# Two places each for the two rotary result tiles, and their high parts as pairs in the pool of the gate's and the convolution's tiles

## The chip, the cores and the metric

One core of a Trainium2 chip runs the whole layer as one program. The metric is the device time of one launch in microseconds (us). The engines are TensorE (PE: matmuls; PEld: its weight loads), VectorE (DVE), ScalarE (ACT), GpSimd (POOL) and SyncE (SP), which here only issues DMAs. Each engine works its instructions off in program order, so an instruction that waits holds up all that stand behind it on its engine. That also holds for DMA issues on SP's queue and on POOL's.

## The reference, cut to what matters

The layer normalizes the input (1024 tokens, 1024 wide), projects it, runs a gated linear attention (GLA) on one half of the columns and a differential attention on the other, joins both by an output projection, then a convolutional feed-forward block, a gated embedding and a last norm. The change lies where queries and keys of the differential attention get their rotary embedding:

```python
def rope(x, pos):
    d = x.shape[-1]
    inv_freq = ROPE_THETA ** (-jnp.arange(0, d, 2, dtype=jnp.float32) / d)
    ang = pos.astype(jnp.float32)[..., None] * inv_freq
    cos, sin = jnp.cos(ang)[:, :, None, :], jnp.sin(ang)[:, :, None, :]
    x1, x2 = xf[..., : d // 2], xf[..., d // 2:]
    return jnp.concatenate([x1 * cos - x2 * sin, x2 * cos + x1 * sin], axis=-1)

q = (rope(q.reshape(B, T, H * 2, dqk), pos) * (dqk ** -0.5)).reshape(B, T, H, 2, dqk)
k = rope(k.reshape(B, T, H * 2, dqk), pos).reshape(B, T, H, 2, dqk)
```

## The kernel before

Every float32 product is made of three matmuls: each operand is split into a high part (rounded to float32r) and a low part (the rest), and `mm3` adds high by high, high by low and low by high.

**A block.** `fm(k, h, evict)` projects the columns of weight block k for half h of the tokens: 24 matmuls (8 slices of 128 rows, three each) into one PSUM tile `psd`, of which there are two. Block n therefore starts only after DVE has read block n - 2.

**A round.** `rotary` (line 534) treats one group of heads (`pr`), queries or keys (`qk`) and one half of the tokens (`h`) at a time: eight rounds, called rounds 1 to 8 here. A round has two blocks, x1 and x2. Of the first, DVE makes `rt0 = x1 cos` (L546) and `rt1 = x1 sin` (L547); of the second `rt2 = x2 sin` (L550) and `rt3 = x2 cos` (L551). POOL makes `rt0 - rt2` in place of rt0 (L552) and `rt3 + rt1` in place of rt3 (L553). These two are the results. ACT rounds each to its high part `rh0`, `rh1` (L560 for queries, L562 for keys), and SP stores it to DRAM (L563); DVE makes the low part in the result's own place (L568, L571), and SP stores that (L572). A round so has four stores of 256 KB, in the order rh0, low part of rt0, rh1, low part of rt3, each to a piece of DRAM of 4 x 32 rows of 512 numbers.

**Places.** rt0, rt2, rt3 and rh0 have one place, rt1 and rh1 share two: six tiles of 2 KB per partition. A tile with one place can be written only when the store of what was in it has landed.

**Weights.** Two raw tiles take the weights from DRAM (L195, 512 KB per block, 20 loads); ACT casts them (L272), DVE makes the low part (L274). The load for block k + 2 is issued when DVE has read block k. Block numbers 4 to 11 are the rounds', 12 to 15 the output gate's, 16 to 19 those of the V projection.

**The gate.** After the rounds, for each of four heads two blocks (k = 12 to 15, halves 0 and 1) give z (L854); ACT applies silu (L861), DVE multiplies with the GLA result `on` (L862), which had been stored to DRAM and is loaded back (L845) into a tile of the tag `c`, of which there are two of 4 KB per partition. The convolution uses this tag much later. ACT and DVE split the product (L866, L867).

**What sets the order.** PE, ACT, DVE and POOL keep the order in which a planner (`Line`, with costs per operation, due times and priorities) calls them. It knows nothing of places. SP's order is set by the tile framework, which places a DMA by when its tile comes free. POOL also issues the loads of the attention's heads (L818, L821), right behind its last L553.

Of the kernel before, what the change touches and what calls it, by code (L numbers as in the profile page):

```python
# [9 lines left out]
F32 = mybir.dt.float32  # L10
F32R = mybir.dt.float32r
# [7 lines left out]
P = 128  # L19
# [24 lines left out]
HALF = 512  # L44
# [85 lines left out]
def kernel(ctx: ExitStack, tc: tile.TileContext, a, out, dbg=None):  # L130
# [17 lines left out]
    wp = ctx.enter_context(tc.tile_pool(name="wp", bufs=2))  # L148
# [37 lines left out]
    wcnt = [0]  # L186
# [39 lines left out]
    with ExitStack() as ph:  # L226
        ph.enter_context(tc.manual_schedule(engines={pe.engine, act.engine, dve.engine, pool.engine}))
        r1 = ph.enter_context(tc.tile_pool(name="r1", bufs=1, side="right"))
# [29 lines left out]
        def prepare(k, delay=3.0, after=()):  # L258

            if k >= len(order) + 4 or k < len(wts):  # L260
                return
            i = k - len(order)
            shape = [P, KB, P] if i < 0 else [P, 2, HALF]
            raw = raw_tile(a["wfm"][order[k]] if i < 0 else a["wtm"][1, i], shape)
            hl = []
            wts.append(hl)

            def hi():
                for nm in ("wh", "wl"):
                    wcnt[0] += 1  # L270
                    hl.append(wp.tile(shape, F32R, name=f"{nm}{wcnt[0]}", tag="w", bufs=8))
                act.copy(hl[0], raw)  # L272
            k_ = line.op("A", T, hi, 2, after, delay)
            line.op("V", T, lambda: dve.tensor_sub(hl[1], raw, hl[0].bitcast(F32)), 2, (k_,), key=("wf", k))  # L274
# [3 lines left out]
        def fm(k, h, evict):  # L278

            n = nf[0]  # L280
            nf[0] += 1
            if n > 1:
                line.need(("fm", n - 2))
            line.need(("wf", k))
            wh, wl = wts[k]
            ps = pd.tile([P, HALF], F32, name="psd", tag="d")
            for kb in range(KB):
                mm3(ps, wh[:, kb], wl[:, kb], xs(xh[h], kb), xs(xl[h], kb), kb == 0, kb == KB - 1)
                line.step(0.69)
                if kb < KB - 1:  # L290
                    yield
            evict(ps, ("fm", n))
            yield
# [224 lines left out]
        with ExitStack() as gs:  # L518
# [15 lines left out]
            def rotary(pr, qk, k):  # L534

                dst = (qs_d, ks_d)[qk]
                for h in range(2):
                    cs = slice(h * HALF, (h + 1) * HALF)
                    t = {}

                    def new(i, t=t):
                        t[i] = r1.tile([P, HALF], F32, name=f"rt{i}", bufs=(1, 2, 1, 1)[i])
                        return t[i]

                    def ev_a(ps, key, t=t, cs=cs, new=new):
                        k_ = line.op("V", HALF, lambda: dve.tensor_mul(new(0), ps, cosr[:, cs]), 1, (("cos",),))  # L546
                        line.op("V", HALF, lambda: dve.tensor_mul(new(1), ps, sinr[:, cs]), 1, (k_,), key=key)  # L547

                    def ev_b(ps, key, t=t, cs=cs, new=new):
                        k1 = line.op("V", HALF, lambda: dve.tensor_mul(new(2), ps, sinr[:, cs]), 1)  # L550
                        line.op("V", HALF, lambda: dve.tensor_mul(new(3), ps, cosr[:, cs]), 1, (k1,), key=key)  # L551
                        ka = line.op("G", HALF, lambda: pool.tensor_sub(t[0], t[0], t[2]), 1, (k1,))  # L552
                        kb_ = line.op("G", HALF, lambda: pool.tensor_add(t[3], t[3], t[1]), 1, (key,))  # L553
                        for x, i, k_ in ((0, 0, ka), (1, 3, kb_)):
                            r_ = {}

                            def hi(x=x, i=i, r_=r_):
                                r_["h"] = r1.tile([P, HALF], F32R, name=f"rh{x}", tag=("rh0", "rt1")[x], bufs=(1, 2)[x])
                                if qk == 0:
                                    act.activation(r_["h"], t[i], AF.Copy, scale=0.125)  # L560
                                else:
                                    act.copy(r_["h"], t[i])  # L562
                                sp.dma_start(dst[4 * pr:4 * pr + 4, 0, x, :, cs], r_["h"].bitcast(F32))  # L563

                            def lo(x=x, i=i, r_=r_):
                                rl = t[i].bitcast(F32R)
                                if qk == 0:
                                    dve.scalar_tensor_tensor(out=rl, in0=t[i], scalar=0.125, in1=r_["h"].bitcast(F32),  # L568
                                                             op0=ALU.mult, op1=ALU.subtract)
                                else:  # L570
                                    dve.tensor_sub(rl, t[i], r_["h"].bitcast(F32))  # L571
                                sp.dma_start(dst[4 * pr:4 * pr + 4, 1, x, :, cs], rl.bitcast(F32))  # L572
                            k_ = line.op("A", HALF, hi, 1, (k_,))
                            line.op("V", HALF, lo, 2, (k_,))
                    prepare(k + 2 + h)
                    yield from fm(k, h, ev_a)
                    yield from fm(k + 1, h, ev_b)
# [1278 lines left out]
    def gate(h, c0, c1, fb, st):  # L1856

        W = c1 - c0
        ng[0] += 1
        if ng[0] > 5:  # L1860
            line.need(("g", ng[0] - 5))
        line.need(("gw", fb))
        if fb % 2 == 0:
            st["pr", fb] = xt([P, 2, HALF], F32)[:, :, 0:W]
            sp.dma_start(st["pr", fb], pp_d[h, fb // 2][:, :, c0:c1])
        psg = pg.tile([P, HALF], F32, name="psg", tag="g")[:, 0:W]
        for kb in range(KB):
            line.need(("v", h, kb))
            vh, vl = vv[h][kb // 2]
            mm3(psg, wg[fb][0][:, kb], wg[fb][1][:, kb], vh[:, kb % 2, c0:c1], vl[:, kb % 2, c0:c1],  # L1870
                kb == 0, kb == KB - 1)
            line.step(W * 3 / 2400)
        return psg, ("g", ng[0])
# [86 lines left out]
    with tc.manual_schedule(engines={pool.engine}):  # L1960
# [38 lines left out]
        for fb in range(4, KB):  # L1999
            x = gate(*part, fb, st)  # L2000
# [90 lines left out]
```

## Time and profile before

| | us |
|---|---|
| median of 3 runs | 1408.72 (1407.35 to 1412.62) |
| the profiled execution: time, span | 1407.91, 1406.0 |
| PE busy in it | 1342.6 |
| DVE, ACT, POOL busy | 922.5, 619.6, 153.1 |
| rounds 1 to 8, first L546 to last | 145.0 to 283.5 |
| gate blocks, end of the last on PE | 330.7 |

The profiled execution lies 0.8 us under the median. PE is the busiest engine, yet a busy PE is not a fast one: matmuls run at the clock that was granted, and the profile gives that clock by stretch. Busy shares are means over stages; which wait ends last in a stage is told by the chain of waits and by the timelines of single engines.

### The profile page before, as it was taken

How to read it: one execution, taken by the hardware profiler on the slowest of the kernel's cores; microseconds unless marked ns; L12 is line 12 of the kernel's file. 1: busy time of each engine (PE TensorE's matmuls, PEld its weight loads, DVE VectorE, ACT ScalarE, POOL GpSimd, SP SyncE). 2: the span in 40 equal slices, each digit the busy share in tenths (PEclk: the TensorE clock that was granted, in tenths of full speed). 3: DMA queues.
4: the chain of work that ended last, by engine and by line, in shares of the span. 5: the costliest groups of instructions: out<-in, count | busy, mean ns of one | idle time of the engine just before them, and what ended most of it. 6: DMA issues, size and time to landing. Idle time of an engine off the chain costs nothing.

```text
span 1406.0 us, 16439 instructions
## 1 busy us (share of the span) xinstructions
PE 1342.6 (95%) x6335; PEld 1076.0 (77%) x6335; DVE 922.5 (66%) x1307; ACT 619.6 (44%) x947; POOL 153.1 (11%) x176
## 2 busy tenths in 40 slices
PE   9999998899999999988999999999999999999996
PEld 6777676676777787756788888888887888887896
DVE  8455653435776777598877778777775363258576
ACT  7434431124664668444554544444554121025444
POOL 0100111120211112320000000000000000013231
PEclk9999999999999999998999999999999999999999
DMA  6101323361658346320222222122275143021222
GB/s 232 31 31 45 98 76 105 96 194 59 190 185 242 118 161 218 123 76 16 90 80 85 90 91 77 73 80 85 91 280 183 61 152 119 15 75 46 83 98 75
DMA packets 49757, 151.87 MB, mean 108 GB/s; under 512 B 5360, under 2 KB 11920, under 8 KB 49680
## 3 DMA queue, kind: packets, MB, share of 16 engines
q1 hardware_dynamic: 45072, 135.10, 28.5%
q0 software_dynamic: 4608, 15.73, 4.2%
q8 instruction: 49, 0.80, 0.2%
q14 instruction: 28, 0.23, 0.0%
HBM read 108.87 MB, written 41.94 MB: 107 GB/s over the span
## 4 chain that ended last, share of the span: by engine, by line
PE 74%; DMA 10%; DVE 9%; ACT 4%; issue 2%; POOL 1%; SPq 1%; DVEq 0%; ACTq 0%; POOLq 0%
PE psu L1441 29%; PE psu L135 14%; PE psg L135 5%; PE psd L135 5%; PE psw L135 4%; PE s L135 3%; PE gps L135 3%; DMA ks_d<-rt 2%; PE psf L135 2%; DMA qs_d<-rt 2%; PE oat L135 2%; PE pst L135 2%; DMA raw<-in_wtm 1%; PE o L135 1%; PE psp L135 1%
## 5 line engine op out<-in xcount | busy, mean ns | idle before, releaser
L1441 PE MATMUL psu<-xt,wt 128*128 128x512 f32 x1008 | 236.9, 390 | 0.0
L1441 PEld LDWEIGHTS psu<-xt,wt 128*128 128x128 f32 x1008 | 189.4, 188 | 40.6
L135 PE MATMUL psd<-xt,wh 128*128 128x512 f32 x512 | 170.8, 416 | 17.7 <-DVE rt L547 12.9
L135 PEld LDWEIGHTS psd<-xt,wh 128*128 128x128 f32 x512 | 96.8, 195 | 44.8 <-issue 14.1
L1441 PE MATMUL psu<-yt,yt 128*128 128x512 f32 x480 | 115.9, 391 | 0.0
L1481 DVE SCALAR_TENSOR_TENSOR c<-s,cwt,c 128x1023 f32<-128x1023 f32 (+1 forms) x88 | 109.2, 1280 | 4.5 <-ACT c L1478 1.9
L1634 DVE TENSOR_TENSOR yt<-yt,psu 128x512 f32<-128x512 f32 x64 | 43.8, 688 | 102.4 <-PE psu L135 102.4
L1441 PEld LDWEIGHTS psu<-yt,yt 128*128 128x128 f32 x480 | 90.0, 188 | 19.4 <-DVE yt L969 0.2
L135 PE MATMUL psd<-xt,wl 128*128 128x512 f32 x256 | 102.8, 401 | 0.0
L135 PE MATMUL psu<-xt,wt 128*128 128x512 f32 x384 | 95.0, 398 | 3.2 <-ACT xt L1620 2.0
L135 PEld LDWEIGHTS psu<-xt,wt 128*128 128x128 f32 x384 | 74.0, 193 | 19.5 <-ACT xt L1620 2.4
L1559 DVE TENSOR_TENSOR s<-s,psu 128x512 f32<-128x512 f32 x60 | 41.1, 686 | 67.9 <-PE psu L1441 67.5
L1551 ACT COPY s<-psu 128x512 f32<-128x512 f32 x80 | 47.0, 588 | 64.1 <-PE psu L1441 60.4
L1776 POOL TENSOR_TENSOR wg<-raw,wg 128x1024 fp32r<-128x1024 f32 x2 | 4.8, 2402 | 627.7 <-ACT wg L1774 627.7
L1478 ACT ACTIVATE c<-s,cwt 128x1024 f32<-128x1024 f32 x44 | 54.8, 1247 | 39.3 <-DVE s L1559 33.7
L1441 PE MATMUL psu<-yt,d 128*128 128x512 f32 x264 | 66.2, 401 | 5.8 <-DVE yt L1385 5.1
L967 ACT CAST wt<-raw 128x1024 fp32r<-128x1024 f32 x42 | 44.3, 1056 | 59.7 <-DVE raw L993 38.2
L1441 PEld LDWEIGHTS psu<-yt,d 128*128 128x128 f32 x264 | 50.7, 193 | 18.3 <-DVE yt L1385 5.5
L1094 ACT ACTIVATE p<-s,nb 128x128 f32<-128x128 f32 (+7 forms) x64 | 47.5, 742 | 30.2 <-DVE nb L1102 28.4
L1102 DVE TENSOR_REDUCE nb<-s 128x1 f32<-128x128 f32 (+7 forms) x64 | 48.3, 755 | 17.6 <-PE s L135 17.2
L135 PEld LDWEIGHTS psd<-xt,wl 128*128 128x128 f32 x256 | 50.1, 196 | 11.2
L135 PE MATMUL psw<-yt,wt 128*128 128x512 f32 x192 | 52.5, 408 | 0.9 <-DVE dvt L1059 0.9
(359 smaller groups left out, 2667.0 us busy)
## 6 DMA issues: line engine op xcount, KB each, us to landing
d<-in_w_up SPq DMA_DIRECT2D x42, 512.0 KB
g_d<-c SPq DMA_DIRECT2D x22, 512.0 KB
raw<-in_w_down SPq DMA_DIRECT2D x22, 512.0 KB
raw<-in_wfm SPq DMA_DIRECT2D x16, 512.0 KB
s<-g_d SPq DMA_DIRECT2D x16, 512.0 KB
yt<-h_d SPq DMA_DIRECT2D x12, 512.0 KB
yt<-ks_d POOLq DMA_DIRECT2D x16, 256.0 KB, 10.3
xt<-ks_d POOLq DMA_DIRECT2D x16, 256.0 KB, 8.0
```

The costliest lines, as they stand in the source:

```text
L135: return pe.matmul(o, l, r, start=start, stop=stop)
L967: act.copy(hl[0], src())
L1094: act.activation(p[:, 0:W], s[:, 0:W], AF.Exp, bias=nb, accum_out=ssum[:, mp:mp + 1])
L1102: k_ = line.op("V", W, lambda: dve.tensor_reduce(out=nb, in_=s[:, 0:W], op=ALU.max, axis=AX.X, negate=True), 2)
L1441: pe.matmul(ps, l[:, c + kb], r[:, kb % 2], start=(kb, i) == (0, 0) and not more, stop=(kb, i) == (3, 2), skip_group_check=more)
L1478: act.activation(c_[i], S[n, i], AF.Identity, scale=cwt[:, blk, 2:3], bias=cwt[:, blk, 3:4])
L1481: k_ = line.op("V", T * 1.05, lambda d=d: dve.scalar_tensor_tensor(out=c_[i][:, d:T], in0=S[n, i][:, 0:T - d], scalar=cwt[:, blk, 2 - d:3 ...
L1551: act.copy(S[n, i][:, lo:lo + HALF], ps)
L1559: dve.tensor_add(o, o, ps)
L1634: line.op("V", HALF, lambda: dve.tensor_add(hblk(h, fb), hblk(h, fb), ps), 0, key=key)
L1776: line.op(lo_eng, T, lambda: (pool if lo_eng == "G" else dve).tensor_sub(wg[fb][1], raws[fb], wg[fb][0].bitcast(F32)), 3, (k_,), key=("gw" ...
```

## The change

The tiles rt0 and rt3 get two places each. rt1 no longer shares with rh1 and gets one, rt2 keeps one: six places as before. The high parts leave this pool: a round takes one tile of tag `c`, 2 x 512 numbers per partition, and rh0 and rh1 are its halves. The tag keeps its two places, which the gate's `on` tiles use too.

```diff
-                        t[i] = r1.tile([P, HALF], F32, name=f"rt{i}", bufs=(1, 2, 1, 1)[i])
+                        t[i] = r1.tile([P, HALF], F32, name=f"rt{i}", bufs=(2, 1, 1, 2)[i])
...
-                                r_["h"] = r1.tile([P, HALF], F32R, name=f"rh{x}", tag=("rh0", "rt1")[x], bufs=(1, 2)[x])
+                                if x == 0:
+                                    wcnt[0] += 1
+                                    t["h"] = wp.tile([P, 2, HALF], F32R, name=f"rh{wcnt[0]}", tag="c", bufs=2)
+                                r_["h"] = t["h"][:, x]
```

Lines behind the diff move by three (L568 becomes L571, L571 becomes L574, L572 L575, L845 L848). The order of PE, DVE, ACT and POOL is the same, instruction by instruction; what differs there are the waits. On DVE, in round 2 before (rt_1463 and rt_1547 are its two results; a DMAHW semaphore is that of a DMA that SP issued):

```order
L546 TENSOR_TENSOR rt_1463<-psd,cosr 128x512 [waits DMAHW5_49,DVE_49,PE_49]
L568 SCALAR_TENSOR_TENSOR rt_1325<-rt_1325,rh_1374 128x512 [waits Pool_49]
L547 TENSOR_TENSOR rt_1471<-psd,sinr 128x512
L550 TENSOR_TENSOR rt_1536<-psd,sinr 128x512 [waits PE_49]
L551 TENSOR_TENSOR rt_1547<-psd,cosr 128x512 [waits DMAHW7_49]
```

The same in the changed kernel:

```order
L546 TENSOR_TENSOR rt_1462<-psd,cosr 128x512 [waits PE_49]
L571 SCALAR_TENSOR_TENSOR rt_1325<-rt_1325,rh_1345 128x512 [waits Pool_49]
L547 TENSOR_TENSOR rt_1470<-psd,sinr 128x512
L550 TENSOR_TENSOR rt_1535<-psd,sinr 128x512 [waits PE_49]
L551 TENSOR_TENSOR rt_1546<-psd,cosr 128x512
```

In round 2 the waits for the stores of round 1 are gone; from round 3 on L546 and L551 wait for the stores of the round before the last.

On SP, the end of the rounds and the loads behind it, before (raw_2263 and raw_2330 are weight blocks 16 and 17, on_2257 the gate's third head; on_2110 and on_2174, the first two, stand far ahead, before the first rh store):

```order
L195 DMA raw_2192<-in_wfm 128x1024
L572 DMA ks_d<-rt_2021 4x32x512
L563 DMA ks_d<-rh_2092 4x32x512
L572 DMA ks_d<-rt_2061 4x32x512
L563 DMA ks_d<-rh_2097 4x32x512
L572 DMA ks_d<-rt_2088 4x32x512
L195 DMA raw_2263<-in_wtm 128x1024
L195 DMA raw_2330<-in_wtm 128x1024
L845 DMA on_2257<-on_d 128x1024
```

The same place in the changed kernel (raw_2255 and raw_2322 are blocks 16 and 17; rh_2085 is the pair of round 8, rt_2015 the second result of round 7):

```order
L195 DMA raw_2184<-in_wfm 128x1024
L575 DMA ks_d<-rt_2015 4x32x512
L848 DMA on_2102<-on_d 128x1024
L566 DMA ks_d<-rh_2085 4x32x512
L575 DMA ks_d<-rt_2054 4x32x512
L566 DMA ks_d<-rh_2085 4x32x512
L575 DMA ks_d<-rt_2081 4x32x512
L195 DMA raw_2255<-in_wtm 128x1024
L848 DMA on_2166<-on_d 128x1024
L195 DMA raw_2322<-in_wtm 128x1024
L848 DMA on_2249<-on_d 128x1024
```

The loads of `on` for the first two heads now stand among the last stores: on_2102 waits until round 7's pair is stored, on_2166 until round 8's is.

## Rows read from the trace of the kernel before

**Rows 1.** The page: the chain that ended last, by engine and line

```profile
PE 74%; DMA 10%; DVE 9%; ACT 4%; issue 2%; POOL 1%; SPq 1%; DVEq 0%; ACTq 0%; POOLq 0%
PE psu L1441 29%; PE psu L135 14%; PE psg L135 5%; PE psd L135 5%; PE psw L135 4%; PE s L135 3%; PE gps L135 3%; DMA ks_d<-rt 2%; PE psf L135 2%; DMA qs_d<-rt 2%; PE oat L135 2%; PE pst L135 2%; DMA raw<-in_wtm 1%; PE o L135 1%; PE psp L135 1%
```

**Rows 2.** The chain, 140 to 340 us: start, length, what

```profile
167.06 6.84 DMA qs_d<-rt
...
215.56 13.20 DMA ks_d<-rt
...
280.24 10.14 DMA ks_d<-rt
...
295.81 19.97 DMA raw<-in_wtm
...
319.52 11.15 PE psd L135 x48
```

**Rows 3.** Timeline of DVE: start, length, operation, idle before and its end

```profile
174.03 0.69 DVE L546 TENSOR_TENSOR rt<-psd,cosr 128x512 f32<-128x512 f32 x1 [4.97 <-DMA qs_d<-rt]
...
267.91 0.69 DVE L546 TENSOR_TENSOR rt<-psd,cosr 128x512 f32<-128x512 f32 x1 [3.88 <-DMA qs_d<-rt]
...
275.96 0.69 DVE L551 TENSOR_TENSOR rt<-psd,cosr 128x512 f32<-128x512 f32 x1 [6.17 <-DMA qs_d<-rt]
...
283.47 0.69 DVE L546 TENSOR_TENSOR rt<-psd,cosr 128x512 f32<-128x512 f32 x1 [3.38 <-DMA ks_d<-rt]
...
309.69 1.23 DVE L862 TENSOR_TENSOR on<-on,yt 128x1024 f32<-128x1024 f32 x1 [1.13 <-ACT yt L861]
316.95 1.23 DVE L274 TENSOR_TENSOR wl<-raw,wh 128x1024 fp32r<-128x1024 f32 x1 [6.03 <-ACT wh L272]
```

**Rows 4.** Timeline of PE, the same columns

```profile
176.57 1.14 PE L135 MATMUL gms<-gsq,ones_r 128*128 128x512 f32 x2 [3.25 <-DVE on L754]
...
220.44 0.73 PE L135 MATMUL psd<-xt,wh 128*128 128x512 f32 x2 [2.19 <-DVE rt L547]
...
319.52 0.70 PE L135 MATMUL psd<-xt,wh 128*128 128x512 f32 x2 [0.81 <-DVE yt L854]
```

**Rows 5.** SP's issues: start, length, transfer

```profile
210.20 0.51 SPq L563 DMA_DIRECT2D ks_d<-rh  x1
...
277.28 0.51 SPq L572 DMA_DIRECT2D ks_d<-rt  x1
...
280.24 0.91 SPq L572 DMA_DIRECT2D ks_d<-rt  x1
...
293.59 0.51 SPq L563 DMA_DIRECT2D ks_d<-rh  x1
```

**Rows 6.** Windows: length, busy of PE, PEld, DVE, ACT, POOL; clock, DMA share, GB/s

```profile
176.57:186.54 9.97, 9.97 (x40) 7.26 (x41) 5.89 (x10) 2.49 (x5) 1.81 (x5) 0.66 0.19 52
144.76:151.84 7.08, 6.91 (x41) 4.93 (x40) 5.42 (x10) 2.49 (x5) 0.80 (x4) 1.00 0.55 186
229.00:233.00 4.00, 3.31 (x15) 2.75 (x16) 3.98 (x4) 0.62 (x1) 1.67 (x1) 1.00 0.15 26
246.30:249.00 2.70, 2.70 (x13) 2.25 (x12) 2.05 (x2) 0.63 (x1) 0.37 (x1) 1.00 0.22 30
249.00:261.70 12.70, 8.65 (x37) 6.60 (x36) 3.69 (x6) 1.58 (x2) 2.31 (x2) 1.00 0.36 117
261.70:264.00 2.30, 2.30 (x11) 1.88 (x11) 2.30 (x2) 0.63 (x1) 0.65 (x1) 1.00 0.22 27
277.30:280.00 2.70, 2.70 (x13) 2.22 (x12) 2.70 (x2) 0.62 (x1) 1.11 (x1) 1.00 0.17 20
285.00:291.70 6.70, 6.10 (x26) 4.75 (x27) 1.59 (x3) 0.62 (x1) 1.75 (x2) 1.00 0.26 91
292.70:295.50 2.80, 2.80 (x14) 2.32 (x13) 1.64 (x2) 2.54 (x3) 2.80 (x6) 1.00 0.23 36
295.50:316.50 21.00, 21.00 (x94) 17.39 (x93) 7.75 (x10) 5.18 (x7) 2.99 (x8) 1.00 0.95 255
```

## The prediction

> **What bounds the kernel now.** I read the chain of waits on the page first. Nearly all of it is TensorE, with two entries of 2% each that are stores of the rotary results [rows 1]: about 56 of 1406 us in which the end of the program hangs on a DMA. The chain in order of time shows where. One piece lies in round 2, at 167 us. Then five follow one another, one per round, from 215.56 to 280.24 us, of 10 to 13 us each, and behind them stands the load of weight block 16 with 20 us [rows 2]. DVE's timeline shows what the stores hold: L546 and L551 stand idle until a store has landed, since rt0 and rt3 have one place [rows 3]. PE waits little by that view, some 2 us at a time, for L547 or L551 [rows 4], but two blocks take it 11.15 us (48 matmuls at full clock) [rows 2], and a round took 15.6 us (from L546 at 267.91 to the next at 283.47 [rows 3]). So PE could go faster by 4.4 us a round if nothing else stood in the way.
>
> Whether something does is to be read from the windows. Between the raw loads the DMA share is flat at 0.26 with 91 GB/s while stores run [rows 6]. A queue that sends on all 16 engines would show more; 0.25 is four of 16. So the stores run on a quarter of the DMA engines, and "26% busy" is full for them. The four stores of a round and its raw load took 12.7 us in a busy stretch (249.0 to 261.7); then come 2.3 to 4 us in which the share is 0.15 to 0.23 but only 20 to 36 GB/s flow, five times after 229 us [rows 6]. These gaps are the start of a store on an empty queue: rt0's low part is issued at 277.28 [rows 5], and bytes flow from 280.0 on. 12.7 and 2.7 make up the round's 15.6. The stage is thus bound by the store queue, and a part of this bound is that the queue runs dry once per round.
>
> The Trainium skill says the same of the quarter ("DMA: Bandwidth & Descriptors", section "Why a DMA increments its semaphore by 16 and not by 1"): a DMA uses the largest number of engines up to 16 that divides the outermost sizes, which for a destination of 4 x 32 x 512 is 4. The trace agrees with 0.26.
>
> **The change part by part.** Nothing is added to or taken from PE, DVE, ACT or POOL, and no transfer is added. What changes are waits, and SP's order.
>
> *Round 2.* L546 waits no longer (4.97 us on DVE [rows 3]). Behind it on DVE stands the L754 that PE's `gms` waits for: 3.25 us of PE [rows 4]. After that wait PE's clock was at its lower level: 40 PE instructions took 9.97 us at a mean clock of 0.66, the like stretch of round 1 took 7.08 us at 1.00 [rows 6]: 2.9 us. With the wait gone both go: -6.1 us for all that follows, the start of the store stream included (round 3's first store, at 210.20 [rows 5], comes at 204.1).
>
> *Rounds 3 to 8.* L546 and L551 wait for the stores of the round before the last, and ACT's first high part for the pair of that round. When L551 is let go, all five transfers of the last round are still queued, some 12.7 us of work; its own stores follow within about 5 us (POOL, ACT, DVE). The queue no longer runs dry. I take the five gaps as gone: 4.0 + 2.7 + 2.3 + 2.7 + 2.8 = 14.5 us [rows 6]. The bounds are nothing (the gaps belong to each store) and all that PE could gain (first rival). I take 14.5, since inside the busy stretches stores follow one another with no such gap.
>
> *rt1 with one place.* L547 must find L553 of the round before done. DVE's own low part of that round, which depends on L553, stands ahead of it; nothing.
>
> *The loads of on.* Two were issued before the first store of the rounds and now go into the stream. At the 255 GB/s of the crowded stretch [rows 6] 512 KB take 2.06 us, two 4.1 us. SP also waits in front of each: the first until round 7's pair has landed, with round 8's four stores and block 16 queued behind it; the second until round 8's pair has landed, with block 17 behind it. In the first wait one store of the stream (the low part of round 7's second result) is still running, in the second that of round 8 and block 16; so I add no gap, and keep what it costs if this cover is missing for the last rival.
>
> *What is late next.* Block 16: DVE works L862, L274 (block 16) and L854 in this order, and PE's last two gate blocks wait for that L854 [rows 3, 4]. Today block 16 lands at 315.78 (295.81 + 19.97 [rows 2]), and PE starts at 319.52, 3.7 us later. It was queued behind the stores. So PE's gain in the rounds is worth only what the stream itself gains up to this landing; with the second head's `on` now behind block 16, that is 315.78 - 6.1 - 14.5 + 4.1 = 299.3, and PE's last two gate blocks start at 303.0: -16.5 us. PE has to wait there, as it will be done with its other gate blocks: from its start on block 8 (220.44 - 2.19 = 218.25 [rows 4], less 6.1) 14 blocks of 5.58 us end at 290.2. After such a wait I expect the lower clock once, and take the 2.9 us of round 2: **-13.6 us**. Everything behind hangs on these blocks and shifts along.
>
> That a load waits behind earlier stores of the same queue is also what the Trainium skill says (same page, section "Queues, rings and completion order": on each DMA engine descriptors are taken in ring order). The trace agrees: 19.97 us for block 16, where the crowded stretch would move 512 KB in about 2.
>
> The sum: 1407.9 (the profiled execution's time) - 13.6 = **1394 us**; the median of the runs lies 0.8 us higher, which I leave out.
>
> **The rivals.**
>
> *PE becomes the bound.* If the queue, once never empty, moves faster than in the stretches seen, PE alone sets the pace and starts its last gate blocks at 290.2 instead of 319.52: -29.3, 1379 us. For it: 4.4 us a round are free on PE, and the busy stretches hold a raw load that slows the stores. Against it: 12.7 us of a busy stretch are already more than PE's 11.15 [rows 2, 6]. By the skill's figure of some 27 GiB/s per DMA engine (same page, section "Specifications") the four engines would be done with a round in an estimated 10.2 us (262 KB of stores and 33 KB of the raw load each), below PE's 11.15, which is this rival; the rows show 12.7.
>
> *The stream stays as long as it is.* If the gaps belong to each round's stores (a pause that the queue makes whatever stands behind), only round 2 is won, two loads are added and PE's lower clock is paid: -6.1 + 4.1 + 2.9 = +0.9, 1409 us: PE waits in one lump instead of in many. For it: the five gaps are alike. Against it: each begins just when the round's second store is issued on an empty queue [rows 5, 6].
>
> *The loads of on come last (slower).* SP issues the second head's load only when round 8's second high part has landed. That store is issued at 293.59 [rows 5]; with the 13.20 us of the longest [rows 2] and 6.1 us earlier it lands at 300.7. If the load then takes as long as block 16 did beside the heads' loads, 19.97 us, L862 of this head starts at 320.7 where it started at 309.69 [rows 3], PE's last gate blocks start at 324.4 and run 2.9 us longer: +7.8, 1416 us. It decides from an issue at 292.9 us on (319.52 - 3.7 - 2.9 - 19.97). Against it: the heads' loads start with the last L553, before round 8's stores are through, and should be done by then.
>
> *The change does not do what it says.* The tiles could still wait, for the pair's first half when the second is written, or for places of other tiles: 1408. The instruction order shows the waits of round 2 gone and none on the pair's second half, so little speaks for it.
>
> **How the numbers follow.** Forecast 0.50, with a range of its own from 1390 (no lower clock) to 1402 (half of the gaps stay); PE as the bound 0.18; the stream as long as before 0.20; the loads last 0.09; nothing changed 0.03. No measurement of this kernel tells less than 0.5% (7 us) from no change. Faster by more than that: the forecast but for 0.04 at its upper end, and PE as the bound: 0.64. Within: 0.04 + 0.20 + 0.03 = 0.27. Slower: 0.09. The range from 1379 to 1410 leaves half of the PE case and the slow one outside, 0.18.
>
> **What would show it.** Right: in round 2 no idle time before L546 and a full clock from 173 to 184 us; a DMA share that does not fall under 0.2 from round 4 to round 8, with no stretch of 2 us under 40 GB/s; L546 to L546 about 13 us; PE idle in one or two lumps of several us before its last four gate blocks, with `on` or block 16 as what was waited for. Wrong: L546 still 15.6 us apart (the stream stays as it is), rounds of 11 us with PE never waiting (PE is the bound), or a wait of DVE at the second L862 that lasts beyond 316 us (slower).

## The result: 1394.3 us, 1.0% faster

| | before | changed |
|---|---|---|
| median of 6 runs each, us | 1408.03 (1401.75 to 1416.86) | 1394.33 (1385.87 to 1399.98) |
| ratio of the runs | | 0.9899, 95% interval 0.9876 to 0.9922 |
| profiled execution, us (span) | 1407.91 (1406.0) | 1385.87 (1384.2) |

The profiled execution of the changed kernel is the shortest of its six, 8.5 us under their median; the first experiment profiles one near the median. In the chain on the page the stores of rt are gone (10% of the span was DMA [rows 1], now 6%). A store of rh and the load of `on` stand there instead:

```profile
PE 80%; DVE 8%; DMA 6%; ACT 4%; issue 2%; POOL 1%; SPq 0%; DVEq 0%; ACTq 0%; POOLq 0%
PE psu L1444 30%; PE psu L135 14%; PE psd L135 9%; PE psg L135 5%; PE psw L135 4%; PE s L135 3%; PE gps L135 3%; PE psf L135 2%; PE oat L135 2%; PE pst L135 2%; PE o L135 1%; DMA ks_d<-rh 1%; PE psp L135 1%; DMA on<-on_d 1%; PE tp L1128 1%
```

The chain from 140 to 340 us says what this looks like in time. One DMA piece per round [rows 2] has become one stretch of TensorE, and one lump of DMA behind it:

```profile
202.94 44.26 PE psd L135 x195
...
253.80 17.90 DMA ks_d<-rh
271.77 12.51 DMA on<-on_d
...
288.07 23.90 PE psd L135 x96
```

DVE's timeline, which answers to [rows 3]: L546 of round 2 starts without idle time, from round 4 on the rounds are 9.6 to 11.5 us apart (two of them here), and the wait that is left is that of the heads' L865 (L862 before) for `on`:

```profile
171.12 0.69 DVE L546 TENSOR_TENSOR rt<-psd,cosr 128x512 f32<-128x512 f32 x1
...
242.16 0.69 DVE L546 TENSOR_TENSOR rt<-psd,cosr 128x512 f32<-128x512 f32 x1 [0.22 <-DMA qs_d<-rt]
...
253.66 0.69 DVE L546 TENSOR_TENSOR rt<-psd,cosr 128x512 f32<-128x512 f32 x1 [0.83 <-DMA qs_d<-rt]
...
284.36 1.23 DVE L865 TENSOR_TENSOR on<-on,yt 128x1024 f32<-128x1024 f32 x1 [14.69 <-DMA on<-on_d]
...
297.06 1.23 DVE L865 TENSOR_TENSOR on<-on,yt 128x1024 f32<-128x1024 f32 x1 [7.93 <-DMA on<-on_d]
```

On PE the many waits of 2 us [rows 4] are one of 8.25 us, before the last four gate blocks:

```profile
288.07 1.19 PE L135 MATMUL psd<-xt,wh 128*128 128x512 f32 x2 [8.25 <-DVE yt L857]
```

SP's issues (start, length, transfer) tell why `on` is late. SP stands from 260.2 to 271.77 in front of L848 until round 7's pair has landed, with round 8's stores queued behind it; the second `on` goes out at 291.88:

```profile
206.48 0.51 SPq L566 DMA_DIRECT2D ks_d<-rh  x1
...
257.58 2.64 SPq L575 DMA_DIRECT2D ks_d<-rt  x1
271.77 0.33 SPq L848 DMA_DIRECT2D on<-on_d  x1
272.20 0.51 SPq L566 DMA_DIRECT2D ks_d<-rh  x1
...
291.88 0.33 SPq L848 DMA_DIRECT2D on<-on_d  x1
```

The windows that answer to [rows 6] (length, busy of PE, PEld, DVE, ACT, POOL; clock, DMA share, GB/s): full clock in round 2; stores alone at a share of 0.26 with 100 to 103 GB/s (91 in the row of the kernel before) and no gap; the heads' loads at 1.02; and half the clock, the 1.2 GHz level, after the lump.

```profile
173.00:184.00 11.00, 10.76 (x63) 7.66 (x61) 6.83 (x13) 4.55 (x9) 2.52 (x6) 1.00 0.29 110
245.00:248.00 3.00, 3.00 (x15) 2.49 (x14) 0.69 (x1) 0.00 (x0) 0.01 (x1) 1.00 0.26 100
254.00:257.00 3.00, 3.00 (x15) 2.45 (x15) 0.94 (x2) 0.00 (x0) 0.00 (x0) 1.00 0.26 103
263.00:279.00 16.00, 16.00 (x73) 13.23 (x72) 2.91 (x4) 4.01 (x4) 4.58 (x11) 1.00 1.02 247
286.00:292.00 6.00, 3.93 (x9) 3.14 (x10) 3.12 (x5) 1.81 (x3) 0.00 (x0) 0.50 0.48 168
```

### The profile page after: what moved, and what is told of

Read it like the earlier page. It is cut to its first block, busy times and chain, and to the rows that moved or that the text cites. A ratio compares the mean times of both kernels' runs of the same rounds, so it can differ in the third digit from the quotient of the medians.

```text
span 1384.2 us, 16433 instructions
## 1 busy us (share of the span) xinstructions
PE 1332.7 (96%) x6335; PEld 1071.2 (77%) x6335; DVE 921.2 (67%) x1307; ACT 618.3 (45%) x947; POOL 151.0 (11%) x176
## 4 chain that ended last, share of the span: by engine, by line
PE 80%; DVE 8%; DMA 6%; ACT 4%; issue 2%; POOL 1%; SPq 0%; DVEq 0%; ACTq 0%; POOLq 0%
PE psu L1444 30%; PE psu L135 14%; PE psd L135 9%; PE psg L135 5%; PE psw L135 4%; PE s L135 3%; PE gps L135 3%; PE psf L135 2%; PE oat L135 2%; PE pst L135 2%; PE o L135 1%; DMA ks_d<-rh 1%; PE psp L135 1%; DMA on<-on_d 1%; PE tp L1128 1%
## 5 line engine op out<-in xcount | busy, mean ns | idle before, releaser
L135 PE MATMUL psd<-xt,wh 128*128 128x512 f32 x512 | 165.9, 405 | 8.2 <-DVE yt L857 8.2
L1105 DVE TENSOR_REDUCE nb<-s 128x1 f32<-128x128 f32 (+7 forms) x64 | 48.3, 754 | 17.0 <-PE s L135 16.6
```

Of the source, the lines that this page charges most:

```text
L135: return pe.matmul(o, l, r, start=start, stop=stop)
L1105: k_ = line.op("V", W, lambda: dve.tensor_reduce(out=nb, in_=s[:, 0:W], op=ALU.max, axis=AX.X, negate=True), 2)
```

## The experiments

Each interval is that of the ratio to the kernel before, run on the same chip in the same job.

### The changed kernel once more (e1_again)

No edit.

> The changed kernel once more, for a second profile: the profiled execution of the first (1385.9 us) was the shortest of six, the median was 1394.3. My theory: the rounds and the gate look the same as in the first profile (rounds 10.9 to 11.5 us apart, one wait of PE of about 8 us before its last four gate blocks), the time is 1392 to 1398, and what differs between two executions lies behind 330 us, at places where TensorE's granted clock is low. Rival: the gain itself swings, because the rounds run at the pace of the stores in some executions (12.7 us and more apart).

Measured: 1391.38 us (1386.87 to 1396.63), a little under the expected range, ratio 0.9867 [0.9826, 0.9908]; the profiled execution took 1394.76 us. The rounds repeat to 0.3 us (60.40 us from L546 of round 3 to that of round 8, 60.10 in the first profile), and the lump to 0.1 (PE waits 8.33 us). What was expected of the difference was wrong: 7.0 of the 8.9 us between the two profiles lie in round 1, not behind 330 us. From its L546 to that of round 2 it took 31.06 us instead of 24.08. There ACT's `sa` (L621) takes the place of `onl` (one tag, L747) and waits until the store of `onl` has landed; in this execution that took 4.64 us from the issue (156.11) to the start of `sa`, in the first profile 2.10. Two timelines, ACT's and PE's, in this execution:

```profile
160.75 0.69 ACT L621 ACTIVATE sa<-psx,vec 128x512 f32<-128x512 f32 x1 [6.90 <-DMA on_d<-onl]
```

```profile
162.53 0.44 PE L135 MATMUL dsp<-gv,kdT 64*64 64x128 f32 x4 [3.29 <-DVE S L726]
```

and what the clock did behind that wait (windows, columns as above):

```profile
150.00:160.00 10.00, 9.06 (x54) 6.51 (x53) 4.76 (x9) 2.49 (x5) 0.79 (x4) 1.00 0.25 95
...
162.00:170.00 8.00, 7.47 (x44) 5.33 (x45) 5.75 (x11) 3.18 (x6) 3.34 (x4) 0.57 0.10 21
170.00:176.00 6.00, 6.00 (x35) 4.10 (x33) 2.07 (x6) 2.04 (x5) 0.40 (x2) 0.72 0.15 60
```

In the first profile the same wait is 0.77 us and the clock stays at 1.00. So a part of what an execution takes depends on how fast this one store lands, and the change has no hand in it.

### The pairs without the second places (e2_pairs_only)

```
-  bufs=(2, 1, 1, 2)[i]
+  bufs=1
```

> The high parts as pairs in the c tiles, but rt0 and rt3 with one place each. My theory: the two places of the results carry the gain; here L546 and L551 wait for the stores of the last round as before, the rounds stay 15 to 16 us apart, the wait of 3.3 us in round 2 is back, and the loads of on come late: 0 to +8 us against the kernel before, 1408 to 1416. Rival: the high parts' places were what held the rounds (rh0 had one place); then the rounds fall to 11 to 13 us and the time to 1392 to 1400.

Measured: 1412.42 us against 1410.75, ratio 1.0007 [0.9983, 1.0032]. L546 and L551 wait as in [rows 3], the rounds take 14.5 to 16.6 us from round 4 on, PE's `gms` waits 3.2 us. Two rows of DVE's timeline:

```profile
268.89 0.69 DVE L546 TENSOR_TENSOR rt<-psd,cosr 128x512 f32<-128x512 f32 x1 [3.36 <-DMA qs_d<-rt]
276.65 0.69 DVE L551 TENSOR_TENSOR rt<-psd,cosr 128x512 f32<-128x512 f32 x1 [5.87 <-DMA qs_d<-rt]
```

The pairs alone give nothing, although rh too has another place and other waits. The gain is that of rt's second places, at least beside the pairs: no run has them without the pairs.

### One second place at a time (e5_rt0_two, e6_rt3_two)

```
-  bufs=(2, 1, 1, 2)[i]
+  bufs=(2, 1, 1, 1)[i]     # e5_rt0_two
+  bufs=(1, 1, 1, 2)[i]     # e6_rt3_two
```

> The changed kernel with two places for rt0 alone (rt3 has one). My theory: round 2's wait goes (-6 us), but L551 still waits until the last store of the round before has landed, the low part of rt0 is made behind it, so the queue still runs dry once a round: rounds 14 to 16 us apart, 1402 to 1411. Rival: any one more place is enough for the queue to stay filled: rounds 11 to 12 us, 1390 to 1398.

> The changed kernel with two places for rt3 alone (rt0 has one). My theory: L546 waits for the second of the four stores of the round before, with two stores and a raw load still queued behind it (some 6 us), and the round's own first stores follow within 5 us, so the queue does not run dry: rounds 11.5 to 13 us apart from round 5 on, though round 2's wait of 3.3 us of PE stays: 1395 to 1403, less than half of the loss of the other single. Rival: both results must have two places for any gain; then it is 1404 to 1412 like the other single.

Measured: two places for rt0 alone 1408.24 us against 1409.06, ratio 0.9984 [0.9954, 1.0015]: nothing, although round 2's wait went as expected (PE's `gms` does not wait). Two places for rt3 alone 1396.45, ratio 0.9918 [0.9886, 0.995]: most of the whole change. The rows show why. With one rt3, L551 waits for the last store of the round before, and when that has landed nothing is queued behind it (DVE's timeline, then windows of the first kernel):

```profile
267.57 0.69 DVE L551 TENSOR_TENSOR rt<-psd,cosr 128x512 f32<-128x512 f32 x1 [8.41 <-DMA qs_d<-rt]
```

```profile
239.00:242.00 3.00, 3.00 (x9) 2.32 (x8) 3.00 (x3) 0.62 (x1) 0.92 (x1) 0.52 0.18 24
...
254.00:257.00 3.00, 3.00 (x15) 2.49 (x14) 3.00 (x4) 0.63 (x1) 0.40 (x1) 1.00 0.29 49
...
269.00:272.00 3.00, 3.00 (x9) 2.37 (x8) 3.00 (x3) 0.63 (x1) 1.00 (x1) 0.53 0.22 38
```

24 to 49 GB/s once a round, and rounds of 14.5 to 15.6 us from round 5 on. Two of these rows show TensorE's clock at its lower level as well; but from 223 to 298 us the chain that ended last holds five stores of 10 to 14 us and no TensorE, so it is not the clock that holds these rounds. With one rt0 it is L546 that waits, for the second of four stores; two more are queued while it does, and bytes keep flowing (the second kernel, the same two views):

```profile
257.47 0.69 DVE L546 TENSOR_TENSOR rt<-psd,cosr 128x512 f32<-128x512 f32 x1 [5.91 <-DMA qs_d<-rt]
```

```profile
242.00:245.00 3.00, 1.75 (x8) 1.13 (x6) 0.23 (x1) 0.00 (x0) 0.00 (x0) 1.00 0.26 94
...
257.00:260.00 3.00, 3.00 (x14) 2.33 (x13) 2.28 (x4) 0.00 (x0) 0.22 (x1) 1.00 0.26 85
```

DVE still waits some 6 us a round, but the rounds take 12.7 to 13.7 us (11.5 to 13 were expected). The gap is made by a wait for the *last* store of the queue, not by waiting as such.

### The other way to the same stores (e3_before_split)

The kernel before, each of the four stores cut so that its outermost size is 32 rows and no longer 4.

```
+  def store(part, x, src, cs=cs):
+      for j in range(4):
+          sp.dma_start(dst[4 * pr + j, part, x, :, cs], src[32 * j:32 * j + 32])
...
-  sp.dma_start(dst[4 * pr:4 * pr + 4, 0, x, :, cs], r_["h"].bitcast(F32))
+  store(0, x, r_["h"].bitcast(F32))
```

> The kernel before, with each store of a round issued as four stores of 32 rows (32 x 512 numbers instead of 4 x 32 x 512), places unchanged. My theory: a store is slow because it runs on a quarter of the DMA engines; cut so that all take part, the DMA share while stores run rises from 0.26 to over 0.5, a store lands 2 to 4 us after its issue instead of 7 to 13, DVE's waits for stores shrink from 55 us to under 15, and the time falls to 1388 to 1400, with one place for each result. Rival: a store's time is a cost of each transfer or of writing to DRAM; then four times as many transfers leave the rounds at 15 us or longer, and the time is 1405 to 1425.

Measured: 1398.50 us (1392.57 to 1400.75), ratio 0.9903 [0.987, 0.9937], with rt0 and rt3 still at one place. DVE's waits for stores fall to 12.8 us in all. Two windows in which only stores run show them on more than a quarter of the engines:

```profile
229.00:232.00 3.00, 3.00 (x15) 2.45 (x15) 1.54 (x3) 0.37 (x1) 0.00 (x0) 1.00 0.61 145
232.00:235.00 3.00, 3.00 (x15) 2.49 (x14) 1.23 (x3) 0.00 (x0) 0.00 (x0) 1.00 0.57 137
```

This bears out the Trainium skill ("DMA: Bandwidth & Descriptors", section "Why a DMA increments its semaphore by 16 and not by 1"), by which the outermost sizes set how many engines a DMA uses: 0.26 with 4, about 0.6 with 32. From round 4 on the rounds take 9.7 to 11.5 us, as in the changed kernel, and here too something else comes late: PE waits 12.5 us before the last gate blocks, for DVE's L274, which waits for the load of block 14. That load stands behind round 8's sixteen stores on SP (DVE's timeline):

```profile
288.92 1.23 DVE L274 TENSOR_TENSOR wl<-raw,wh 128x1024 fp32r<-128x1024 f32 x1 [16.67 <-ACT wh L272]
```

### `on` past the stores (e4_on_pool, e7_on_pool_first)

```
-  sp.dma_start(on, on_d[hd])
+  (pool if hd < 2 else sp).dma_start(on, on_d[hd])     # e4_on_pool; hd == 0 in e7_on_pool_first
```

> The changed kernel, with the loads of on for the first two heads issued on POOL's queue, behind its last addition and ahead of the heads' loads, so that SP does not stand behind the high parts' landing. My theory: round 8's stores and block 16 are issued some 10 us earlier, the first on lands before 272 us, PE's one wait (8.25 us) and the lower clock behind it go: 7 to 11 us less than the changed kernel, 1383 to 1388. Rival: the heads' loads now start only when round 8's pair has landed, and PE waits for them at the first scores instead: no gain, 1392 to 1400.

> The changed kernel with only the first head's load of on issued on POOL's queue, ahead of the heads' loads; PE's order is that of the kernel before (in the run with both loads on POOL one score product of the attention stood ahead of the last 96 gate products and waited 15.9 us). My theory: the first on lands before 274 us, PE's wait of 8.25 us before the last four gate blocks goes, one of 0 to 4 us for the second on comes before the last two: 3 to 8 us less than the changed kernel. Rival: the heads' loads, begun later, are now what PE waits for at the first scores: no gain, within 2 us of the changed kernel.

Measured: 1395.68 us, ratio 0.9897 [0.9857, 0.9938], and 1394.59, ratio 0.9896 [0.9863, 0.9929]: the changed kernel's time, twice. PE's waits from 140 to 345 us with both loads on POOL (us in total, times, longest):

```profile
PE s L135 <- DMA yt<-ks_d: 15.9, 1, 15.9
...
PE dsp L135 <- DVE S L726: 0.8, 1, 0.8
```

POOL stood 11.95 us in front of the second `on`, whose place DVE had not yet freed, with the heads' loads queued behind it, and a score product waits for one of these. (One score product had come to stand ahead of the last 96 gate products here.) With the first `on` alone on POOL, PE's order is the old one; L865 of the first head starts after 6.06 us of waiting instead of 14.7, that of the second after 16.02 instead of 7.9, and PE has its lump two gate blocks later:

```profile
306.61 1.19 PE L135 MATMUL psd<-xt,wh 128*128 128x512 f32 x2 [9.59 <-DVE yt L857]
```

In the changed kernel the DMA engines are full from 263 to 279 us (1.02 above) with the heads' loads, the last stores and `on`. These two runs show what the heads' loads cost the first `on`, since they hold them back behind it. DVE's timeline, L546 of round 8 and the first head's L865, in e4_on_pool and then in e7_on_pool_first:

```profile
251.97 0.69 DVE L546 TENSOR_TENSOR rt<-psd,cosr 128x512 f32<-128x512 f32 x1 [0.86 <-DMA qs_d<-rt]
...
273.08 1.23 DVE L865 TENSOR_TENSOR on<-on,yt 128x1024 f32<-128x1024 f32 x1 [5.29 <-DMA on<-on_d]
```

```profile
260.09 0.69 DVE L546 TENSOR_TENSOR rt<-psd,cosr 128x512 f32<-128x512 f32 x1 [0.86 <-DMA qs_d<-rt]
...
282.06 1.23 DVE L865 TENSOR_TENSOR on<-on,yt 128x1024 f32<-128x1024 f32 x1 [6.06 <-DMA on<-on_d]
```

The first L865 starts 21.1 and 22.0 us after L546 of round 8, and 30.7 in the changed kernel. In both kernels an earlier first `on` made something else late, and nothing was won.

### Cut stores and block 14 with round 8 (e8_split_early14)

The kernel of e3_before_split, and

```
   prepare(k + 2 + h)
+  if k == 10 and h == 1:
+      prepare(14)
```

> The kernel before with its old places, each store cut in four of 32 rows, and block 14's weights prepared with round 8 instead of behind it (in the first run of cut stores its load stood behind all stores, and PE waited 12.5 us for it). My theory: with stores that land within 2 to 5 us no second place is needed: rounds about 11 us apart, no wait of PE over 4 us before the gate's end, on loaded early: 1380 to 1390, less than the changed kernel by 4 to 12 us. Rival: two places are needed all the same, as each round's first product waits for its predecessor's store: rounds over 12.5 us, 1394 to 1404.

Measured: 1390.00 us (1386.80 to 1392.73), ratio 0.9872 [0.985, 0.9895], 8.5 us under the kernel without block 14 moved (from another job). PE's lump is gone but for 2.9 us:

```profile
PE psd L135 <- DVE yt L860: 2.9, 1, 2.9
PE dsp L135 <- DVE S L729: 2.2, 1, 2.2
```

The rounds take 9.9 to 11.5 us from round 4 on with one place each, so no second place is needed, as expected. That this kernel is faster than the changed one isn't shown, since the intervals overlap; its profile had the slow landing of `onl` (3.55 us), with a clock of 0.88 from 140 to 210 us.

### A place for `onl` (e9_own_onl)

The kernel of e6_rt3_two (`onl`'s new place takes the 2 KB that the single rt0 leaves), and

```
-  on[0] = g.tile([P, HALF], F32, name="onl" if e else "on", tag="sa" if e else "on")
+  on[0] = g.tile([P, HALF], F32, name="onl" if e else "on", tag="onl" if e else "on")
```

> The kernel of the run with two places for rt3 alone and one for rt0, in which onl (the result of the odd heads' normalization, L747) also gets a place of its own (2 KB a partition, which the single rt0 leaves) instead of sharing sa's. Every engine has the same instructions in the same order as that run. It asks why executions of one kernel lie some 10 us apart. Theory (the landing of the store on_d<-onl is short or long from execution to execution, about 2.1 us or 3.5 to 4.6 us from its issue to the end of ACT's wait; ACT's sa in round 1 waits for it, PE's dsp waits for that, and when dsp waits over 2 us the granted clock of 140 to 210 us falls to 0.85 to 0.93): no wait of sa for a DMA, PE's wait for S in 140 to 200 us under 0.8 us, clock 1.00 in 140 to 210 us, whatever the landing; the slow end of the executions goes: 1389 us (1386 to 1393), fastest and slowest under 6 us apart, ratio 0.984 to 0.989. Rival (the landing is only a sign of an execution that is slower everywhere, and sa's wait lies beside other work): the wait of sa is gone, but the time stays at 1396 us, ratio 0.991, with executions 8 to 10 us apart.

Measured: 1396.33 us (1395.17 to 1397.14), ratio 0.9906 [0.9886, 0.9927]. Six executions lie within 2.0 us, where the four without the edit lay within 9.9 and the six of the changed kernel within 14.1. No `sa` waits for a DMA any more. So the theory holds for the spread: the shared place made it. It fails for the median, which stayed, and for the clock. L546 of round 2 waits for rt0's one place, PE's `gms` waits 3.33 us, and the clock falls behind that:

```profile
170.00:180.00 10.00, 6.67 (x25) 3.83 (x23) 3.93 (x6) 2.65 (x4) 0.00 (x0) 0.80 0.31 92
180.00:190.00 10.00, 10.00 (x48) 7.53 (x47) 5.37 (x10) 3.38 (x7) 3.32 (x6) 0.69 0.18 63
```

In the profile of e6_rt3_two `gms` waits 3.29 us and the clock stays at 1.00. What makes the one fall and not the other these runs don't tell.

### All three (e10_combined)

The kernel of e9_own_onl with the cut stores and block 14 of e8_split_early14.

> The kernel of e9_own_onl with the stores of the result tiles cut into four of 32 rows each and the weight loads of block 14 issued with round 8 (both as in e8_split_early14). One thing it can't keep: a score product of the first head comes to stand ahead of the last 96 gate products on TensorE, as in e4_on_pool. Theory (three causes that add up: the store queue's pace, the loads of block 14 behind round 8's stores, the wait of sa): L546 to L546 10 to 11 us with store waits under 3 us in all, clock 1.00 in 140 to 210 us, no wait of psd for yt over 3 us: 1383 us (1379 to 1388), ratio 0.979 to 0.984, below every kernel so far. Rival (the score product in front decides): PE's s waits 8 us or more for a head's load (yt<-ks_d or yt<-qs_d) before the last 96 gate products, the clock falls behind it, and the time is 1390 us or more, ratio 0.986 or above.

Measured: 1382.52 us (1380.97 to 1383.41), ratio 0.9806 [0.9785, 0.9826]: the fastest here; its slowest execution lies under the changed kernel's fastest (1385.87). The rounds take 10.0 to 11.9 us from round 4 on and the clock is 1.00 from 140 to 260 us, about as expected. Two things were not: DVE's waits for rt's stores are 0.9 to 2.9 us each and 11.6 in all (under 3 were expected), and PE has a lump of 5.27 us (no wait over 3 was expected):

```profile
285.14 1.19 PE L135 MATMUL psd<-xt,wh 128*128 128x512 f32 x2 [5.27 <-DVE yt L863]
```

The chain has a weight load ahead of this lump (275.33 to 281.41 us), which SP issued only behind its wait for the second `on`'s place. How much each of the three causes gives is not taken apart by this run. The rival's wait of a score product for the heads' loads didn't come, though that product stands in front as in e4_on_pool; there POOL had stood in front of `on`, which here goes through SP.

## Why the prediction was right, and where not

Measured from L546 of round 1 (each step from one L546 to a later one, the last to the end of the last gate product), in us:

| | before | changed, short execution | changed, e1_again |
|---|---|---|---|
| round 1 to 2 | 29.05 | 24.08 | 31.06 |
| round 2 to 3 | 23.26 | 22.44 | 22.44 |
| round 3 to 8 | 86.18 | 60.10 | 60.40 |
| round 8 to the end of the gate | 47.19 | 58.29 | 58.74 |
| sum against before | | -20.8 | -13.0 |

*The number.* 1394 was forecast and 1394.3 measured, but not term by term.

*Round 2: -6.1 forecast.* In the short execution -5.0 and -0.8: L546 doesn't wait, `gms` doesn't wait, and the clock is 1.00 where it was 0.66. The mechanism is shown. In e1_again the same stretch is 1.2 us longer than before, since `sa` waited for a slow store. The prediction took round 1 as given; it is the place where executions of every kernel here differ.

*Rounds 3 to 8: -14.5 forecast.* The fifth of the gaps (292.7 us) lies behind L546 of round 8, so -11.7 answers to this row of the table. This is the term that was mis-sized: -26.1 and -25.8. The gaps went, as forecast (no window of 3 us from 218 to 263 us under 96 GB/s). But the pace of 12.7 us that was put in their place, "since inside the busy stretches stores follow one another with no such gap", was too slow: the busy stretch was itself not full. Windows of the kernel before:

```profile
251.00:254.00 3.00, 0.34 (x2) 0.33 (x3) 1.78 (x3) 0.00 (x0) 0.00 (x0) 1.00 0.26 72
255.00:258.00 3.00, 3.00 (x15) 2.49 (x14) 0.00 (x0) 1.58 (x2) 0.48 (x1) 1.00 0.26 102
270.00:273.00 3.00, 3.00 (x9) 2.32 (x8) 0.00 (x0) 1.57 (x2) 1.16 (x1) 0.50 0.26 103
289.00:291.00 2.00, 1.61 (x8) 0.99 (x6) 0.53 (x1) 0.00 (x0) 0.00 (x0) 1.00 0.26 77
```

So stores moved 102 to 103 GB/s at the share of 0.26 before, too, as they do in the changed kernel, and the 91 of [rows 6] (285.0 to 291.7 us) is a mean over such pieces and the slow one at 289, as the 12.7 us hold the slow one at 251. Why these are slow stays open. 102 GB/s over four engines are 25.5 each. By an estimate from that, a stream that is kept full takes 11.6 us for a round's stores and raw load, not 12.7. The Trainium skill ("DMA: Bandwidth & Descriptors", section "Specifications") has some 27 GiB/s, which made the estimate of 10.2 us a round; the trace differs by 12%. From round 4 on the measured rounds take 9.6 to 11.5 us, around PE's own 11.15. PE is busy without a break from 203 to 279 us, and DVE waits 2.7 us in all for rt's stores, in rounds 7 and 8. Within the rounds the first rival was right: PE is the bound, with the stream close behind. The clock of 0.50 in one of the rows above is no rival cause: from 207 to 319 us the chain of the kernel before holds no TensorE.

*What is late next: +4.1 for two loads and +2.9 for the clock forecast, with the fifth gap +4.2 for the row; +11.1 and +11.6 measured.* That PE would wait in a lump before its last gate blocks, that `on` or block 16 would be the cause, and that the clock would fall once behind it came about. The place was off. The prediction named block 16 behind the second `on`; it was the first `on`. The step said of SP's first wait "I add no gap", and looked at the store queue alone. What it left out is that PE and POOL now run ahead of the stores: POOL issues the heads' loads from 262 us on, right beside that wait, while stores of round 7 are still queued. The pair of round 7 was issued by 256.5 and landed at 271.7, `on` itself took 12.5 us more. With the heads' loads held back (e4_on_pool, e7_on_pool_first) the pair landed 14.7 us after L546 of round 8 instead of 18.1, and the first L865 started 8.7 to 9.6 us earlier: about the size of the lump. Before the change both of these loads of `on` had been issued ahead of the first rh store, and of the transfers in the crowd PE waited for block 16 alone, with 19.97 us [rows 2]. The lump is 8.25 us; the 96 products after it took 23.9 us, and at full clock they take 22.3 (twice 11.15 [rows 2]), so the clock cost 1.6 us, not 2.9 (2.3 in e1_again, with 24.55 us).

*The sum.* In an execution near the median +2.0 - 0.8 - 25.8 + 11.6 = -13.0 stand against -13.6 forecast. Rounds that gained 14 us more than forecast, 7 us more given back behind them, and a round 1 that took 7 us in this execution: the errors cancel, and the hit is in good part luck. Beside these steps lie 2 to 4.6 us more ahead of round 1 and 3.3 to 4.7 us less behind the gate; neither was traced to a cause.

*The rivals.* "The stream stays as long as it is" falls with e6_rt3_two and the windows: the gaps belong to the wait for the last store, not to every store. "The loads of on come last" had the right kind of mechanism and the wrong size: the second L865 waited 7.93 us, until 297.06 and not 320.7. "Does nothing" is what e2_pairs_only does; in the changed kernel L546 of round 2 doesn't wait.

## What to carry to other kernels

When a tile's one place is freed by the last store of a queue, the queue runs dry in each turn, and the start-up comes on top of the transfers; look for the tile whose store is issued last and double that one first. Price a stream that will be kept full by a rate, and ask whether the row it is read from was itself full: here 91 GB/s was a mean over a full stream at 102 and a slower piece at 77. A stage whose engines run ahead of its stores meets the next one's loads, so list every transfer that its end releases and ask which of them a waiting queue now holds back.

## What was not expected of the hardware

The landing of one 256 KB store (`onl`'s), which none of the edits up to e8_split_early14 touches, took 2.1 us from its issue to the start of the instruction that waited for it in five profiles (before, changed, e2, e4, e6), and 3.6 to 4.6 us in five others (e1, e3, e5, e7, e8). What comes late is the end of the transfer. The 2.4 us that begin 2 us after the issue, in the changed kernel, in e1_again and in e9_own_onl:

```profile
155.60:158.00 2.40, 1.63 (x11) 0.92 (x11) 1.58 (x4) 2.04 (x3) 0.00 (x0) 1.00 0.00 0
```

```profile
158.11:160.51 2.40, 1.13 (x5) 0.56 (x4) 0.00 (x0) 0.00 (x0) 0.00 (x0) 1.00 0.05 14
```

```profile
154.77:157.17 2.40, 2.40 (x22) 1.63 (x20) 2.40 (x6) 1.27 (x2) 0.72 (x1) 1.00 0.03 7
```

Where the landing was slow and something waited for it, PE waited 2.2 to 3.3 us and the granted clock from 140 to 210 us was 0.85 to 0.93. In the kernels with two places for rt0 round 1 then took 30.4 to 35.1 us (e1, e5, e7) instead of 24.1 (changed, e4). The third window shows the same trickle where nothing waits any more: with `onl` in a place of its own the fastest and slowest executions of a kernel lie 2.0 and 2.4 us apart (e9, e10), in all the others 6 to 16. What makes the end of this store late stays open.
